# Value projection of the second 512 tokens in f16 high and low parts, K tiles outermost

## The chip, the cores and the metric

The kernel runs on one core of one Trainium2 chip. The metric is the device time of one launch in microseconds (us), where lower is better; times are medians of a few runs. The core has five engines, each of which takes its own instructions strictly in order: TensorE (matmuls; PE in the profile, its weight loads PEld), VectorE (DVE), ScalarE (ACT), GpSimd (POOL) and SyncE (SP). In this kernel SP issues nearly all DMA transfers, one after another, so a transfer that waits for its buffer holds up every later transfer in SP's order.

## The reference

One encoder layer on 1024 tokens of width 1024. A projection feeds two groups of attention heads, each group's output is gated, and an output projection, a residual and a layer norm follow:

```python
h = jnp.einsum('bsd,de->bse', x, w_in[layer])
q_a, k_a, v_a, z_a, q_b, k_b, v_b, z_b = jnp.split(h, SPLIT_POINTS, axis=-1)
y_a = neighborhood_attention(q_a, k_a, v_a, rel_pos_bias[layer])     # 8 heads of 64, 2-D window
y_b = windowed_gqa_with_sink(rotary(q_b), rotary(k_b), v_b, sink_logits[layer])
mixed = jnp.concatenate([y_a * jax.nn.silu(z_a), y_b * jax.nn.silu(z_b)], axis=-1)
y = jnp.einsum('bse,ed->bsd', mixed, w_out[layer])
x = layer_norm(DEEPNORM_ALPHA * x + y, ln_gain[layer], ln_bias[layer])
```

(The reshapes to heads are left out here.) All inputs and outputs are float32. What matters here is the first line, and of its columns the values v_a (512) and v_b (128): x (1024 x 1024) times 640 columns of w_in, called wv in the kernel.

## The kernel before, in words

**Number formats.** A float32 product is made of three products of narrower parts: with x = xh + xl and w = wh + wl, it takes xh wh + xl wh + xh wl. The parts are either fp32r (a rounded float32 that TensorE takes directly; in the profile f32), or f16 after scaling by a power of two that is made from the largest magnitude or the sum of magnitudes of the tensor.

**Value product.** The first stage (lines 402 to 587) computes the values, tokens as output rows, 640 columns in two parts of 320 (index a). K, the inner dimension, is 8 tiles of 128 (index k). x comes transposed, in two halves of 512 tokens; a half has four row tiles of 128 tokens (index t, 0 to 3 in the first half and 4 to 7 in the second). `load_x` and `load_wv` load a K tile into a staging buffer (`xr`, four; `wvr`, three), ACT casts it to the high fp32r part and DVE subtracts to get the low part. `v_mms` issues the three passes for one bank. For the first half k runs outermost over eight PSUM banks (four t by two a). For the second half (line 564) the bank runs outermost: one bank after another takes all 24 matmuls, and `v_out` then copies it on ACT to `v32`. The order of instructions in this stage and up to the output stage is the order in which the code is written (`manual_schedule`), for every engine.

**Scale of x.** The later projections take x in f16. `x_max` takes the largest magnitude of each of 16 x tiles on DVE; `x_scale`, in the second half's second group of matmuls, makes the common scale xsc with the help of a transposing matmul. All 16 x tiles are loaded a second time (`x2_load`), and `x16_part` makes their f16 parts: ACT the high part, and the low part DVE in one instruction or POOL in two.

**Weights of the projections.** Blocks of 128 columns of w_in, each in two halves of four K tiles (index m, block n has halves 2n and 2n+1). `w_load` brings a half into one of five buffers `wr`; `w_scan` sums its magnitudes on ACT; `w_scale(n)` turns the sums of block n into a scale, with a small matmul over the sums (line 222) that waits for both scans; `w_split` makes the f16 parts (ACT high; POOL low in two instructions, lines 201 and 202), and the load of half m+5 waits until POOL is done with half m, as it takes its buffer. Before, `w_split(0)` and `w_split(1)` stand within the second half of the value product (line 585).

**Projections.** `project` (line 355) computes one block for all tokens: two halves of 512 tokens, 24 matmuls of 512 columns each (line 376), alternating between two banks `pj`; ACT evacuates. Beside the first six, `run_to` runs events at fixed counts of matmuls: `v_scale` at 16 (a transposing matmul and small DVE steps for the scale of the values), `v_part(t)` from 30 on (values to f16, and out to DRAM), and `sum_w(i)` at 14, 28 and so on: it sums the magnitudes of a whole later block, loaded by `sum_load` as `ws` (512 KB), on ACT or DVE. The first four `ws` loads follow in SP's order the loads of weight halves 5 and 6. After that the attention runs beside the remaining projections.

Of the kernel before, what the change touches and what calls it, by code (L numbers as in the profile page):

```python
# [7 lines left out]
F32 = mybir.dt.float32  # L8
# [29 lines left out]
X1AT = 4  # L38
# [22 lines left out]
def hybrid_block(ctx, tc, xT, x, wt, wv, wo, bias, sink, gain, lbias, cos, sin, bmask, out):  # L61
# [27 lines left out]
    for half in range(2):  # L89
        for k in range(KT):  # L90
            t = big_tile(f"x{half}{k}")
            xh[half, k], xl[half, k] = t[:, 0, :], t[:, 1, :]
# [20 lines left out]
    xsc = const.tile([128, 1], F32, name="xsc")  # L113
    xrs = const.tile([128, 1], F32, name="xrs")
# [287 lines left out]
    with ExitStack() as vctx:  # L402
        vp = vctx.enter_context(tc.tile_pool(name="vp", bufs=2))
        vw = vctx.enter_context(tc.tile_pool(name="vw", bufs=1))
        wvh, wvl = [], []
        ps = bank("t")
        for _ in range(26):
            nc.tensor.matmul(ps[:, :128], warm, warm, start=True, stop=True)

        def load_x(half, k, cuts=(0, 512)):  # L410
            raw = vp.tile([128, 512], F32, tag="xr", name="xraw", bufs=4)
# [10 lines left out]
        def load_wv(k, cuts=(0, 640)):  # L422
            raw = vp.tile([128, 640], F32, tag="wvr", name="wvraw", bufs=3)
# [10 lines left out]
            for a, b in zip(cuts, cuts[1:]):  # L434
                nc.vector.tensor_sub(l[:, a:b], raw[:, a:b], h[:, a:b].bitcast(F32))
                yield

        def first_tiles():
            xr = vp.tile([128, 512], F32, tag="xr", name="xraw", bufs=4)
            wr = vp.tile([128, 640], F32, tag="wvr", name="wvraw", bufs=3)  # L440
# [16 lines left out]

        def interleave(*gens):
# [4 lines left out]
        def v_mms(ps, t, a, k, passes=(0, 1, 2)):  # L463
            ts = slice(128 * (t % 4), 128 * (t % 4) + 128)
            cs = slice(320 * a, 320 * a + 320)
            for i in passes:
                lh, rh = ((xh, wvh), (xl, wvh), (xh, wvl))[i]
                nc.tensor.matmul(ps[:, :320], lh[t // 4, k][:, ts], rh[k][:, cs],  # L468
                                 start=(k == 0 and i == 0), stop=(k == KT - 1 and i == 2))
# [3 lines left out]
        gm = const.tile([128, 1], F32, name="gm")  # L473

        def x_max(half, k):
            i = 8 * half + k
            nc.vector.tensor_reduce(xm[:, i:i + 1], xh[half, k].bitcast(F32), axis=AXX, op=ALU.max,
                                    apply_absolute_value=True)

        staged = [0]  # L480

        def stage(name):
            tag = ("xr", "xr", "xr", "xr", "wvr", "wvr", "wvr", "vt", "vt", "vt")[staged[0] % 10]
            staged[0] += 1
            if tag == "xr":
                return vp.tile([128, 512], F32, tag="xr", name=name, bufs=4)
            return vp.tile([128, 640], F32, tag=tag, name=name, bufs=3)[:, :512]

        def x_scale():
            ps = bank("t")  # L490
            nc.tensor.transpose(ps[:, :128], gm.to_broadcast([128, 128]), identf)
            nc.vector.tensor_reduce(gm, ps[:, :128], axis=AXX, op=ALU.max)
            nc.vector.tensor_scalar_max(gm, gm, 2.0 ** -16)
# [760 lines left out]
```

## Time and profile before

| | |
|---|---|
| median of 3 runs | 451.86 us (450.78 to 452.11) |
| the profiled execution, its own time | 451.96 us |
| its span in the profile | 450.2 us |
| matmuls | 3290 |
| TensorE busy | 440.9 us (98%) |
| DVE, ACT, POOL busy | 342.8, 301.6, 230.7 us |
| granted TensorE clock, mean | 0.999 of full speed |

In the profile a row of a timeline gives the start and the length in us, the engine, the line of the kernel, the operation, what is written from what is read, and shapes; in brackets stands how long the engine had been idle and what ended that. Matmul lengths overlap, since they are pipelined, so their cost is read from the distance of their starts. Where only the length of a run of equal instructions is given (x13), its share is the length divided by the count. "DMA to landing" is the time from issue to the last byte.

### The profile page before, as it was taken

To read this page: it belongs to the slowest core of one execution; us is meant where nothing else is said; L and a number is where in the kernel's file an instruction comes from. 1 tells how busy PE (TensorE), PEld (TensorE's weight loads), DVE (VectorE), ACT (ScalarE), POOL (GpSimd) and SP (SyncE) were. 2 spreads that over 40 slices of the span, in tenths; PEclk is the share of its full clock that TensorE was granted. 3 is DMA by queue.
4 is the path that set the end of the run, shared out by engine and by line. 5 is a ranking of instruction groups with operands and counts; after the bars stand their busy time and mean duration, and the time that the engine had idled before them with its cause. 6 is when DMAs were issued, how large, how long until landed. Compare 5 with 4: busy or idle time off the path is not lost.

```text
span 450.2 us, 9537 instructions
## 1 busy us (share of the span) xinstructions
PE 440.9 (98%) x3290; PEld 264.2 (59%) x3290; DVE 342.8 (76%) x833; ACT 301.6 (67%) x686; POOL 230.7 (51%) x241
## 2 busy tenths in 40 slices
PE   8999999999999999999999999999999999999994
PEld 8999974444445565555555555656556654444453
DVE  4787956628987797897888887888778837679944
ACT  4648649776489977787867888788778946302401
POOL 0003943555838558768506667765493504305740
PEclk9999999999999999999999999999999999999999
DMA  7898277975649999697778899989999988203611
GB/s 238 278 313 295 87 256 232 336 266 221 202 106 216 194 177 175 126 154 146 138 143 181 166 176 162 225 189 190 195 182 247 190 169 333 79 0 99 228 71 71
DMA packets 135281, 83.88 MB, mean 186 GB/s; under 512 B 101440, under 2 KB 113600, under 8 KB 134976
## 3 DMA queue, kind: packets, MB, share of 16 engines
q1 hardware_dynamic: 135088, 83.13, 76.9%
q8 instruction: 26, 0.43, 0.4%
q14 instruction: 23, 0.19, 0.1%
q10 hardware_dynamic: 144, 0.13, 0.1%
HBM read 52.83 MB, written 9.96 MB: 139 GB/s over the span
## 4 chain that ended last, share of the span: by engine, by line
PE 79%; DVE 6%; ACT 5%; issue 4%; DMA 3%; POOL 1%; SPq 0%; DVEq 0%; ACTq 0%; POOLq 0%
PE ps_pj L376 37%; PE ps_s L960 9%; PE ps_s L468 6%; PE ps_pj L960 5%; PE ps_t L810 5%; PE ps_t L960 5%; PE ps_pj L468 3%; PE ps_t L468 3%; PE ps_s L745 3%; PE ps_s L746 3%; ACT split L781 1%; DMA tr<-split 1%; DVE split L782 1%; ACT ps_s L771 1%; DMA wor<-in_wo 1%
## 5 line engine op out<-in xcount | busy, mean ns | idle before, releaser
L376 PE MATMUL ps_pj<-xf,wh 128*128 128x512 f16 x672 | 202.1, 379 | 0.3 <-DVE ks L260 0.3
L376 PE MATMUL ps_pj<-xf,wl 128*128 128x512 f16 x336 | 127.3, 379 | 0.0
L376 PEld LDWEIGHTS <-wh 128*128 128x128 f16 x672 | 63.6, 98 | 60.6 <-DVE ks L260 0.6
L771 ACT ACTIVATE ps_s<-sn,nm 128x385 f32<-128x385 f32 (+3 forms) x128 | 70.1, 548 | 28.4 <-DVE nm L755 28.0
L782 DVE SCALAR_TENSOR_TENSOR split<-ps_s,split 128x384 f16<-128x384 f32 (+2 forms) x128 | 65.7, 513 | 28.1 <-ACT split L781 26.4
L960 PEld LDWEIGHTS <-m 128*128 128x128 f16 x432 | 40.1, 98 | 41.1 <-DVE m L868 0.2
L781 ACT ACTIVATE split<-ps_s 128x384 f16<-128x384 f32 (+2 forms) x128 | 57.8, 452 | 3.3 <-DMA tr<-split 0.9
L376 PEld LDWEIGHTS <-wl 128*128 128x128 f16 x336 | 32.8, 98 | 37.4
L201 POOL TENSOR_SCALAR wr<-wr,wsc 128x512 f32<-128x512 f32 x26 | 20.7, 795 | 42.6 <-ACT wh L196 36.2
L960 PE MATMUL ps_s<-wo,m 128*128 128x512 f16 (+1 forms) x192 | 40.8, 366 | 0.0
L755 DVE CUSTOM_DVE_ANT_0 sn<-ps_s,bm,nsk 128x384 f32<-128x384 f32 (+1 forms) x64 | 40.6, 635 | 0.3
L745 PE MATMUL ps_s<-ks,qs 128*128 128x384 f16 (+4 forms) x128 | 39.2, 306 | 0.6 <-DVE qs L260 0.3
L755 DVE CUSTOM_DVE_ANT_0 sn<-ps_s,bias,sg 128x264 f32<-128x264 f32 (+1 forms) x64 | 35.0, 548 | 5.7 <-PE ps_s L746 2.7
L746 PE MATMUL ps_s<-ks,qs 128*128 128x384 f16 (+4 forms) x128 | 39.2, 306 | 0.0
L810 PEld LDWEIGHTS <-tr 128*128 128x128 f16 (+1 forms) x1104 | 36.7, 98 | 3.2 <-DMA tr<-split 0.6
L202 POOL TENSOR_TENSOR wl<-wr,wh 128x512 f16<-128x512 f32 x26 | 32.7, 1256 | 2.2
L717 POOL TENSOR_SCALAR bias<-bias,rsg 128x552 f32<-128x552 f32 (+1 forms) x24 | 19.1, 798 | 27.3 <-DMA bias<-in_bias 16.7
L292 POOL COPY ks<-ks 64x512 f16<-64x512 f16 x40 | 26.1, 661 | 7.3 <-DVE ks L260 2.8
L468 PE MATMUL ps_s<-wvh,x 128*128 128x320 f32 x128 | 29.8, 313 | 0.0
L1015 ACT ACTIVATE sd<-mv,eps 128x1 f32<-128x1 f32 x8 | 2.4, 294 | 36.0 <-DVE mv L1013 34.6
L1059 POOL TENSOR_TENSOR xr<-xr,gb 128x512 f32<-128x512 f32 x7 | 9.8, 1397 | 32.4 <-ACT xr L1056 32.4
L960 PE MATMUL ps_pj<-wo,m 128*128 128x512 f16 (+1 forms) x144 | 26.2, 326 | 0.0
(169 smaller groups left out, 823.4 us busy)
## 6 DMA issues: line engine op xcount, KB each, us to landing
xraw<-in_xT SPq DMA_DIRECT2D x31, 256.0 KB, 4.7
ws<-in_wt SPq DMA_DIRECT2D x15, 512.0 KB, 6.0
wr<-in_wt SPq DMA_DIRECT2D x26, 256.0 KB, 3.3
wor<-in_wo SPq DMA_DIRECT2D x22, 256.0 KB, 3.4
bias<-in_bias SPq DMA_DIRECT2D x16, 276.0 KB, 3.3
xr<-in_x SPq DMA_DIRECT2D x8, 512.0 KB, 9.6
out<-xr SPq DMA_DIRECT2D x15, 256.0 KB, 2.2
bias<-in_bias SPq DMA_DIRECT2D x8, 368.0 KB, 3.8
```

Of the source, the lines that this page charges most:

```text
L202: nc.gpsimd.tensor_sub(l, raw, h)
L292: nc.gpsimd.tensor_copy(t[o, sl], t[a, sl])
L376: nc.tensor.matmul(ps, a[:, k % 4, :], mv, start=(k == 0 and i == 0), stop=(k == KT - 1 and i == 2))
L468: nc.tensor.matmul(ps[:, :320], lh[t // 4, k][:, ts], rh[k][:, cs], start=(k == 0 and i == 0), stop=(k == KT - 1 and i == 2))
L745: nc.tensor.matmul(ps[:, :m], q, sl[0], start=True, stop=False)
L746: nc.tensor.matmul(ps[:, :m], q, sl[1], start=False, stop=True)
L755: nc.vector.tensor_tensor_reduce(sn[:, :m], ps[:, :m], bias_t, sg[:, c:c + 1], init, op0=ALU.add, op1=ALU.min, accum_out=nm)
L771: nc.scalar.activation(pt[:, :m], sn[:, :m], AF.Exp, bias=nm, scale=-1.0, accum_out=sm[:, k:k + 1])
L781: nc.scalar.activation(hl[:, :m, 0, :c], src, AF.Copy, scale=PSCALE)
L782: nc.vector.scalar_tensor_tensor(hl[:, :m, 1, :c], src, PSCALE, hl[:, :m, 0, :c], op0=ALU.mult, op1=ALU.subtract)
L810: nc.tensor.matmul(ps[:, HD * m:HD * m + HD], a, b_, start=(i == 0), stop=(i == len(mms) - 1))
L960: nc.tensor.matmul(ps, lh[:, ts], rh[:, cs], start=(e == EO[0] and i == 0), stop=(e == EO[-1] and i == 2))
```

## The change

- The four row tiles of the second half are multiplied from f16 parts: of x (`x16h`, `x16l`, the same ones that the projections use), and of wv (`wv16`, new, kept in the buffers of the gates z). The result is multiplied by the product of both units, `vdq`, in `v_out`.
- x's second half is loaded once, straight into its big tiles as float32 (`x1_load`), and never cast to fp32r. Its f16 parts are made from there. Of the first half, K tiles 4 to 7 stay in their staging buffers until their f16 parts are made, and tiles 0 to 3 are loaded again (`x0_again`).
- wv: six staging buffers instead of three, so that tiles 2 to 7 stay; tiles 0 and 1 are loaded again (`wv_again`). `wv_sum` sums the magnitudes of each tile on ACT; `wv_hi` (ACT) and `wv_lo` (DVE) make the f16 parts. For tiles 2, 4, 6 and 7 the low fp32r part moves from DVE to POOL.
- Both scales are made ahead of the second half, by `pow2` on DVE alone, in place of `x_scale` and its matmul.
- In the second half k runs outermost, in the order `KO`, over six banks (row tiles 4, 5 and 7); row tile 6 follows, two banks one after another.
- In the first half the passes run outermost over the four row tiles (k from 1 to 6), and x is loaded ahead of wv.
- `w_split(0)` and `w_split(1)` and the f16 parts of x's first tiles 1 to 3 stand in the last two groups of matmuls; the loads of cos and sin move behind the value product.

```diff
-X1AT = 4
+KO = (2, 3, 4, 5, 6, 7, 0, 1)
+X1_AT = ((), (), (0,), (1,), (2, 3), (4, 5), (6, 7), ())
...
+        def wv_stage(k):
+            nst[0] += 1
+            return vp.tile([128, 640], F32, tag=("wvr", "vt")[(nst[0] - 1) // 3 % 2], name="wvraw", bufs=3)
...
-                nc.vector.tensor_sub(l[:, a:b], raw[:, a:b], h[:, a:b].bitcast(F32))
+                (nc.gpsimd if k in (2, 4, 6, 7) else nc.vector).tensor_sub(l[:, a:b], raw[:, a:b], h[:, a:b].bitcast(F32))
...
+        def wv_sum(k):
+            nc.scalar.activation(junk[:, :640], wvh[k].bitcast(F32), AF.Abs, accum_out=wvm[:, k:k + 1])
...
-                lh, rh = ((xh, wvh), (xl, wvh), (xh, wvl))[i]
-                nc.tensor.matmul(ps[:, :320], lh[t // 4, k][:, ts], rh[k][:, cs],
-                                 start=(k == 0 and i == 0), stop=(k == KT - 1 and i == 2))
+                if t < 4:
+                    lh, rh = ((xh[0, k], wvh[k]), (xl[0, k], wvh[k]), (xh[0, k], wvl[k]))[i]
+                else:
+                    (xa, xb), (wa, wb) = (x16h[1, k], x16l[1, k]), wv16[k]
+                    lh, rh = ((xa, wa), (xb, wa), (xa, wb))[i]
+                ko = KO if t >= 4 else range(KT)
+                nc.tensor.matmul(ps[:, :320], lh[:, ts], rh[:, cs],
+                                 start=(k == ko[0] and i == 0), stop=(k == ko[-1] and i == 2))
...
+        def pow2(c, parts, op, least):
...
+            nc.vector.tensor_reduce(g, parts, axis=AXX, op=op)
+            nc.vector.tensor_copy(ta, g.to_broadcast([128, 32]))
+            nc.vector.transpose(tb, ta)
+            for b in range(4):
+                nc.vector.tensor_reduce(m4[:, b:b + 1], tb[32 * b:32 * b + 32], axis=AXX, op=ALU.max)
+            nc.vector.tensor_reduce(g[:32], m4, axis=AXX, op=ALU.max)
+            nc.vector.tensor_scalar_max(g[:32], g[:32], least)
+            nc.vector.tensor_scalar(g[:32].bitcast(I32), g[:32].bitcast(I32), 0x7F800000, None, op0=ALU.bitwise_and)
+            for b in range(4):
+                nc.vector.tensor_scalar_mul(unit[32 * b:32 * b + 32, c:c + 1], g[:32], 2.0 ** -14)
+            nc.vector.reciprocal(runit[:, c:c + 1], unit[:, c:c + 1])
...
+        def wv_hi(k):
+            nc.scalar.activation(wv16[k][0], wraw[k], AF.Copy, scale=wvs)
+
+        def wv_lo(k):
+            h, l = wv16[k]
+            nc.vector.scalar_tensor_tensor(l, wraw.pop(k), wvs, h, op0=ALU.mult, op1=ALU.subtract)
+            if k in (2, 3):
+                wv_again(k - 2)
...
-            if k in (1, 3) or (half, k) == (0, 5):
+            if k % 2 == 0:
                 nc.gpsimd.tensor_scalar(raw, raw, xsc, 1.0, op0=ALU.mult, op1=ALU.mult)
                 nc.gpsimd.tensor_sub(l, raw, h)
             else:
                 nc.vector.scalar_tensor_tensor(l, raw, xsc, h, op0=ALU.mult, op1=ALU.subtract)
+            if not half and k >= 4:
+                x0_again(k - 4)
...
+            for j in X1_AT[k]:
+                x1_load(j)
+            wv_sum(k)
+            x_max(0, k)
+            for j in X1_AT[k - 1] if 0 < k < 7 else ():
+                x_max(1, j)
...
+        pow2(1, wvm, ALU.add, 2.0 ** -30)
+        x_max(1, 6)
+        x_max(1, 7)
+        pow2(0, xm, ALU.max, 2.0 ** -16)
+        nc.vector.tensor_mul(vdq, unit[:, 0:1], unit[:, 1:2])
+
+        def ahead(i):
+            if i < KT:
+                k = KO[i]
+                wv_lo(k)
+                x16_part(1, k)
+                if i + 2 < KT:
+                    wv_hi(KO[i + 2])
+
+        wv_hi(KO[0])
+        wv_hi(KO[1])
+        ahead(0)
+        for i in (0, 2, 6, 1):
+            v_out(banks[i], i // 2, i % 2)
+        ahead(1)
+        for i in (3, 7):
+            v_out(banks[i], i // 2, i % 2)
+        ahead(2)
+        for i in (4, 5):
+            v_out(banks[i], i // 2, i % 2)
         for m in range(5):
             w_load(m)
...
+        for i, k in enumerate(KO):
+            ahead(i + 3)
+            if 1 <= i < 5:
+                w_scan(i - 1)
+            if i >= 3:
+                x16_part(0, (i + 1) % KT)
+            for a in range(2):
+                for t in (0, 1, 3):
+                    v_mms(part[2 * t + a], 4 + t, a, k)
+            if i in (4, 6):
+                w_scale(i // 2 - 2)
+            if i >= 4:
+                v_max(i - 4)
+        for t in (0, 1, 3):
+            for a in range(2):
+                v_out(part[2 * t + a], 4 + t, a)
...
+        for a in range(2):
+            ps = bank(tags[4 + a])
+            for k in KO:
+                v_mms(ps, 6, a, k)
+            if a == 0:
+                x16_part(0, 1)
+                w_split(0)
+                x16_part(0, 2)
+                v_max(4)
+            else:
+                x16_part(0, 3)
+                v_max(5)
+                v_max(7)
+                w_split(1)
+            v_out(ps, 6, a)
+        v_max(6)
...
         at(16, v_scale)
+        at(20, table_load, "cos", cos, "zc")
+        at(20, table_load, "sin", sin, "zs")
```

115 lines of the change are left out of this document (39 added, 76 removed).

## The prediction

> **What bounds the kernel now.** I read the page's busy shares first, then the chain that ended last (by engine, then in order of time), then the windows of the two stretches which the change touches: the second row block of the value product (33.29 to 61.90) and the first two projections behind it. In a window row the columns are length, busy time of PE, PEld, DVE, ACT and POOL with their counts, granted clock, DMA share and GB/s.
>
> ```profile
> span 450.2 us, 9537 instructions
> PE 440.9 (98%) x3290; PEld 264.2 (59%) x3290; DVE 342.8 (76%) x833; ACT 301.6 (67%) x686; POOL 230.7 (51%) x241
> PE 79%; DVE 6%; ACT 5%; issue 4%; DMA 3%; POOL 1%; SPq 0%; DVEq 0%; ACTq 0%; POOLq 0%
> ...
> 55.02 7.04 PE ps_s L468 x48
> 71.26 10.38 PE ps_pj L376 x48
> ...
> 33.29:61.90 28.61, 28.61 (x197) 28.17 (x195) 23.97 (x43) 17.90 (x37) 16.64 (x14) 1.00 0.59 194
> 61.90:82.50 20.60, 20.60 (x100) 9.49 (x99) 13.60 (x28) 18.57 (x33) 8.70 (x8) 1.00 0.86 277
> ```
>
> TensorE is busy in 98% of the span and holds 79% of the chain. In the value product 48 matmuls of 320 columns take 7.04 us, 146.7 ns each; in a projection 48 of 512 columns take 10.38, 216.2 ns each. No other engine ends a wait in either stretch, but ACT is busy in 18.57 of 20.60 us right behind the value product. So time can be won by cheaper matmuls, and any wait that TensorE gets here is paid in full, because it works without slack up to the tail.
>
> ```profile
> 8.08 0.31 PE L468 MATMUL ps_pj<-wvh,x 128*128 128x320 f32 x1
> 8.70 0.41 PE L468 MATMUL ps_pj<-wvh,x 128*128 128x320 f32 x1 [0.31 <-DVE x L419]
> ...
> 33.29 0.46 PE L468 MATMUL ps_pj<-wvh,x 128*128 128x320 f32 x2
> ...
> 61.90 0.60 PE L376 MATMUL ps_pj<-xf,wh 128*128 128x512 f16 x2
> ...
> 71.09 0.17 PE L222 MATMUL ps_t<-wm,ones 128*128 128x2 bf16 x1
> ```
>
> These are TensorE's own marks: its one wait in the first row block (8.08 to 8.70, for the low part of x's second K tile), the end of the first block (33.29), the first projection (61.90), and the small matmul that sums the statistics of the third weight block (71.09, 9.19 after 61.90).
>
> **Removed: time per matmul.** The second block's 192 matmuls change from fp32r to f16. The trace has no f16 matmul of 320 columns; it has 384 and 512.
>
> ```profile
> 200.48 0.33 PE L745 MATMUL ps_s<-ks,qs 128*128 128x384 f16 x1
> 200.64 0.33 PE L746 MATMUL ps_s<-ks,qs 128*128 128x384 f16 x1
> 200.81 0.59 PE L376 MATMUL ps_pj<-xf,wh 128*128 128x512 f16 x2
> ...
> L376 PEld LDWEIGHTS <-wh 128*128 128x128 f16 x672 | 63.6, 98 | 60.6 <-DVE ks L260 0.6
> L468 PEld LDWEIGHTS ps_s<-wvh,x 128*128 128x128 f32 x128 | 21.8, 190 | 0.0
> ```
>
> 384 columns start 0.16 to 0.17 us apart, 512 columns 0.216; the line through both gives 137 ns for 320. Weight loads are no obstacle: 98 ns in f16, 190 in fp32 (there they are longer than the matmul spacing, and overlap only in part). 192 x (146.7 - 137) = 1.86 us saved. Bounds: 2.6 (133 ns, if spacing goes with columns from 0.16 at 384) and 0 (if nothing but columns counted before).
>
> The Trainium skill (TensorE: Matmul & The Clock Gate, "Back-to-back issue gap") gives a sustained 131 ns for 512 columns and 81 for 128; by it 320 columns would cost about 106 ns, an estimate, and the saving would be near 7.8 us. The 216.2 ns measured here for 512 columns contradict it, so this stays out of the sum.
>
> In the first block x is now loaded ahead of wv, and all four row tiles take the high pass before the low one, so the low part of tile 1 has four matmuls more to arrive. The 8.70 start becomes 8.08 + 0.15: 0.47 us saved (0 to 0.47), and the first block ends near 32.8. The eight casts and eight subtractions of x's second half go away on ACT and DVE, which costs or saves nothing by itself, beside TensorE's work; the one matmul that made x's scale goes too, uncounted.
>
> **Added: a wait between the blocks.** Before, the second block needed only x's fp32r parts; the common scale of x was made beside it. Now every second-block matmul needs the scales of x and wv first. DVE must finish the subtraction of x's last first-half tile, then seven maxima, the power-of-two chain of wv, the last two maxima, and the same chain for x; then ACT casts tile 2, and POOL makes its low part, which the very second matmul needs.
>
> ```profile
> 18.00:20.00 2.00, 2.00 (x16) 2.00 (x15) 1.90 (x3) 1.89 (x4) 0.00 (x0) 1.00 0.48 179
> ...
> 20.82 0.62 ACT L416 CAST x<-xraw 128x512 fp32r<-128x512 f32 x1
> 33.13 0.79 ACT L526 COPY v<-ps_t 128x320 f32<-128x320 f32 x2
> 39.61 2.56 ACT L514 ACTIVATE xf<-xraw,xsc 128x512 f16<-128x512 f32 x4 [0.80 <-DVE xsc L496]
> ...
> 18.84 1.89 DVE L419 TENSOR_TENSOR x<-xraw,x 128x512 fp32r<-128x512 f32 x3
> 30.05 7.80 DVE L477 TENSOR_REDUCE xm<-x 128x1 f32<-128x512 f32 x13
> 40.37 0.75 DVE L519 SCALAR_TENSOR_TENSOR xf<-xraw,xsc,xf 128x512 f16<-128x512 f32 x1 [0.79 <-ACT xf L514]
> 43.34 0.15 DVE L225 TENSOR_SCALAR wg<-wg 128x1 int32<-128x1 int32 x1
> 43.53 0.15 DVE L226 TENSOR_SCALAR wsc<-wg 128x1 int32<-128x1 int32 x1
> 43.60 0.20 DVE L227 TENSOR_SCALAR inv<-wg,xrs 128x1 f32<-128x1 f32 x1
> 73.14 0.88 DVE L607 SCALAR_TENSOR_TENSOR vt<-v,vrs,vt 128x640 f16<-128x640 f32 x1
> ...
> 41.05 0.69 POOL L516 TENSOR_SCALAR xraw<-xraw,xsc 128x512 f32<-128x512 f32 x1 [39.74 <-ACT xf L514]
> 41.83 1.56 POOL L517 TENSOR_TENSOR xf<-xraw,xf 128x512 f16<-128x512 f32 x1
> 45.61 1.13 POOL L516 TENSOR_SCALAR xraw<-xraw,xsc 128x512 f32<-128x512 f32 x1
> 63.24 0.69 POOL L201 TENSOR_SCALAR wr<-wr,wsc 128x512 f32<-128x512 f32 x1 [4.98 <-ACT wh L196]
> 64.02 1.16 POOL L202 TENSOR_TENSOR wl<-wr,wh 128x512 f16<-128x512 f32 x1
> ```
>
> The tile k=7 was cast at 20.82. Two more x tiles go ahead of it in SP's order and wv of k=7 goes behind, while the loads no longer wait for three staging slots (at 18 to 20 the queue moved 179 GB/s at half load); I put the subtraction at 20.8 (19.9 to 22.0). It takes 0.63 (1.89 for three), seven maxima 0.60 each (7.80 for 13): 25.6. ACT's column sums of wv are done by then: two casts and a sum are about 3 x 0.8 = 2.4 us a tile (0.64 from 2.56 for four, times 640/512), while TensorE spends 24 x 146.7 = 3.5 on one. A power-of-two chain is nine dependent small steps, 0.19 apart (43.34 to 43.53), and six independent ones at 0.07 (43.53 to 43.60): 2.1; with the 32-wide copy and transpose, for which no row stands, 2.2 (2.1 to 15 x 0.19 = 2.85). So 27.8, two maxima 29.0, second chain 31.2. ACT's cast: 0.64 (2.56 for four): 31.85. POOL: 0.78 from 41.05 to 41.83 and 1.56: 34.2. Its bounds are 1.94 (63.24 to 64.02, plus 1.16) and 2.77 (1.13, 0.08 between, 1.56), because DVE runs the two wv low parts beside it.
>
> TensorE could go on at 32.8. The first matmul finds its bank, scale and high parts about in time; the second waits until 34.2: **1.3 us lost** (0 to 4.2 with all bounds on one side). Behind it one K tile is 18 x 137 = 2.47 us of TensorE; each needs from ACT two casts of 0.64 and 0.8, from DVE a 640-wide product-subtract (0.88) and every second time a 512-wide one (0.75), from POOL every second time 2.34. All fit, DVE even if they stretch by half. The eight bank evacuations are placed just ahead of the banks' use. These operations cost nothing as long as that cover holds; without it each would delay a K tile by its own length.
>
> **Moved: the first two weight splits, and what stands behind them on SP.** Before, they were made amid the second block. Now they stand in its last 6.6 us (48 matmuls for row tile 6). On SP the loads of weight halves 5 and 6 wait for them (slots of halves 0 and 1), and behind those wait the first four whole-block loads for the statistics (ws), then everything later on SP, cos and sin included. ACT, in order, takes the sum over ws 0, then an activation table load, the evacuation of the first projection bank and the sum of weight half 5; TensorE's small matmul needs that last one.
>
> ```profile
> 56.37 2.26 SPq L185 DMA_DIRECT2D wr<-in_wt  x2
> 59.01 1.93 SPq L623 DMA_DIRECT2D ws<-in_wt  x4
> ...
> DMA to landing us min/median/max: 3.7/5.2/6.9
> ...
> 64.27 1.04 ACT L631 ACTIVATE junk<-ws 128x1024 bf16<-128x1024 f32 x1
> 65.42 1.28 ACT L335 ACT_TABLE_LOAD   x1
> 67.41 0.69 ACT L335 ACTIVATE z<-ps_pj,inv 128x512 f32<-128x512 f32 x1 [0.70 <-PE ps_pj L376]
> 68.60 1.53 ACT L615 ACTIVATE vt<-v,vrs 128x640 f16<-128x640 f32 x2
> ```
>
> When the six-bank loop ends, ACT still has about 1.0 us of evacuations (0.79 for two), one x cast 0.64 and the weight cast 0.64: POOL starts at 2.3. Weight half 0: 1.94; x tile 2: 2.34; half 1: 1.94; done at 8.5, 1.9 us into the projection (1.4 to 3.6). Before, SP had both loads out at 56.37 + 2.26 = 58.63, 3.3 us ahead of the projection. TensorE itself needs half 1 only at 14 x 0.216 = 3.0. The ws issue follows about 0.8 later, at 2.7: the issue of half 6 (0.48 at the most, the pitch of the four) and 0.38 (58.63 to 59.01). Landing takes 3.7 at the least and 5.2 in the middle; only one transfer is ahead, so 4.1: 6.8 (before: issue 2.9 us ahead of the projection, so it was there when ACT came at 64.27). ACT then needs 65.42 - 64.27 = 1.15, 1.28 of table load, and 68.60 - 67.41 = 1.19: 3.6 in all, and TensorE may go on at 10.4. It gets there at 9.2: **1.2 us lost** (0.3 to 4). Further sums wait less: the other ws loads follow at 0.48 (1.93 for four), and ACT and TensorE are late together.
>
> The copies saved or added in DMA (12 x reloads fewer, two wv reloads more, cos and sin after the value product) lie beside TensorE's work; without that cover one load is worth its issue-to-landing time once, 3.7 to 5.2 by the row above.
>
> **Sum.** -1.86 - 0.47 + 1.3 + 1.2 = +0.2 us against the profiled execution's 451.96 (span 450.2 and 1.76 around it), which lies 0.10 over the median of 451.86. Forecast for the median: **452.1**, its own range 450.8 to 453.3.
>
> **Rivals.**
> 1. Both waits are hidden: the loads come 1 us earlier, and ws lands in 3.7 behind clean POOL work. Then only the savings stay: 451.86 - 2.3 = 449.5. For it: loads no longer stall on slots. Against: DVE's queue is fixed work from 21 on, and half 1 cannot be split earlier. With the first wait alone gone, 450.8.
> 2. Slower: the scale of x comes late. Start at 22.0, chains at 2.85, POOL at 2.77 give +2.9: 455.0. It decides as soon as x's scale is later than about 30 (then POOL's part is late), and from there each us costs one. For it: 30 small steps stand on one engine. A middle form is POOL fully blocked by each of DVE's two 0.88 us operations: 1.94 + 1.76 = 3.7 instead of 2.34, time 453.5. Against: clean and contended rows differ by 0.44 and 0.40, not by 0.88. The Trainium skill (SBUF — State Buffer, "Who interferes with whom") has just this exclusive lock between VectorE and GpSimd, the loser blocking for the whole instruction; the rows bear it out in direction only.
> 3. The second wait is longer, with ws landing 5.2 after issue and POOL contended: +2.7, 454.8.
> 4. The f16 matmul is no faster: 454.0. Against it stands the weight-load row.
>
> **How the numbers follow.** About 0.3% (1.36 us) is what a measurement can tell from no change. Forecast 0.43, rival 1 0.15 (half of it only partly so), rival 2 0.22, rival 3 0.15, rival 4 0.05. Faster by over 0.3% (below 450.5): 0.12 of rival 1 and 0.06 of the forecast's edge, 0.18. Slower (above 453.2): most of rivals 2 to 4, 0.38. Same: 0.44. Range 449.9 to 455.0.
>
> **What would show it.** Right: second-block matmuls 137 ns apart; TensorE's idle before the second one released by POOL's low part of tile 2, 1 to 2 us; the first projection at 60 to 61; idle before the statistics matmul released by ACT, with ACT's idle before the sum over ws ended by a DMA. Wrong: 147 ns spacing; a gap released by ACT's evacuation or by x's scale alone; no gap 9.2 us into the projections; a loss beyond 90 us.

## The result, and the profile after

| | kernel before | changed kernel |
|---|---|---|
| median, measured side by side | 451.10 us (448.43 to 452.17, 22 runs) | 452.43 us (449.89 to 455.62, 22 runs) |
| ratio | 1 | 1.0038 (95% interval 1.0020 to 1.0057) |
| profiled execution, its own time | 451.96 us | 455.62 us |
| its span | 450.2 us | 453.6 us |

The change costs 1.3 us in the median. It also widens the spread, and the profiled execution is the longest of its 22, so its trace shows more loss than a usual execution has. A second one is read below beside it. The page of the changed kernel:

```profile
span 453.6 us, 9544 instructions
PE 440.8 (97%) x3289; PEld 255.9 (56%) x3289; DVE 343.3 (76%) x851; ACT 308.0 (68%) x702; POOL 241.7 (53%) x251
PEclk9996999999999999999999999999999999999999
```

TensorE is busy as long as before, in a longer span, and the row of granted clocks, which was even before, has a 6 in its fourth slice. TensorE's timeline shows the marks that the prediction used:

```profile
32.60 0.31 PE L486 MATMUL ps_s<-wvl,x 128*128 128x320 f32 x1
35.78 0.34 PE L486 MATMUL ps_pj<-wq,xf 128*128 128x320 f16 x1 [2.87 <-ACT v L560]
37.39 0.71 PE L486 MATMUL ps_pj<-wq,xf 128*128 128x320 f16 x2 [1.27 <-POOL xf L546]
...
59.48 6.68 PE L486 MATMUL ps_t<-wq,xf 128*128 128x320 f16 x48
66.00 0.59 PE L379 MATMUL ps_pj<-xf,wh 128*128 128x512 f16 x2
...
76.63 0.16 PE L225 MATMUL ps_t<-wm,ones 128*128 128x2 bf16 x1 [1.29 <-ACT junk L219]
```

The last matmul of the first block starts at 32.60, so the block ends about 0.15 later, at 32.75 (before: 33.29). Then TensorE waits 2.87 us for ACT's evacuation of bank 0, does one matmul, and waits 1.27 for POOL's low part of x: 4.14 us between the blocks. Row tile 6's 48 matmuls take 66.00 - 59.48 = 6.52 us, 135.8 ns each. From the second matmul of the block to the first projection pass 66.00 - 37.39 = 28.61 us, where 191 matmuls at 135.8 ns need 25.94: 2.67 us are lost with no wait shown. The windows (length, PE busy, granted clock, DMA share, GB/s) say where:

```profile
35.50:36.00 0.50, 0.22 (x1) 0.91 0.54 97
36.00:42.50 6.50, 5.22 (x21) 0.50 0.94 318
42.50:43.00 0.50, 0.50 (x5) 0.77 0.34 111
```

The mean of 0.91 in the first window puts the fall to half clock at 35.91 us, and the mean of 0.77 in the last puts its end at 42.73. TensorE works through 5.34 us of that, from 37.39 on, and half of 5.34 is the 2.67. The statistics matmul, which stood at 71.09 before, is at 76.63: 5.54 us late. That is -0.54 (first block) - 2.1 (192 matmuls at 146.7 - 135.8 ns) + 4.14 + 2.67 + 1.29 = 5.5. The span is only 3.4 us longer, so 2.1 us come back further on.

Why the scale of x is late stands in the timelines of VectorE, GpSimd and ScalarE:

```profile
20.94 1.57 POOL L445 TENSOR_TENSOR wvl<-wvraw,wvh 128x640 fp32r<-128x640 f32 x1 [1.58 <-ACT wvh L442]
21.02 2.04 DVE L429 TENSOR_TENSOR x<-xraw,x 128x512 fp32r<-128x512 f32 x1
22.98 4.23 DVE L494 TENSOR_REDUCE xm<-x 128x1 f32<-128x512 f32 x7
27.14 0.14 DVE L504 TENSOR_REDUCE g<-wvm 128x1 f32<-128x8 f32 x1
27.77 0.74 DVE L508 TENSOR_REDUCE m<-tb 32x1 f32<-32x32 f32 x4
29.08 0.62 DVE L513 TENSOR_SCALAR unit<-g 32x1 f32<-32x1 f32 x4
33.73 0.16 DVE L514 RECIPROCAL runit<-unit 128x1 f32<-128x1 f32 x1
...
33.98 0.72 ACT L543 ACTIVATE xf<-x,runit 128x512 f16<-128x512 f32 x1 [2.50 <-issue]
34.61 0.81 ACT L524 ACTIVATE wq<-wvraw,runit 128x640 f16<-128x640 f32 x1
35.33 0.40 ACT L560 COPY v<-ps_pj 128x320 f32<-128x320 f32 x1
...
34.80 1.30 POOL L545 TENSOR_SCALAR x<-x,runit 128x512 f32<-128x512 f32 x1 [12.29 <-ACT xf L543]
36.18 1.15 POOL L546 TENSOR_TENSOR xf<-x,xf 128x512 f16<-128x512 f32 x1
```

VectorE's last subtraction of x takes 2.04 us. POOL's subtraction of wv began 0.08 us before it and ends at 22.51; VectorE ends 0.55 after that. The seven maxima end at 27.14, each chain of small steps takes 2.7 us, and x's scale is there at 33.8. ACT makes x's high part and another tile of wv, and then first evacuates bank 0, though that bank was full before 31. POOL's low part is ready at 37.33.

The second wait, on SP, POOL and ACT:

```profile
64.34 4.59 SPq L188 DMA_DIRECT2D wr<-in_wt  x2
67.42 1.16 POOL L205 TENSOR_TENSOR wl<-wr,wh 128x512 f16<-128x512 f32 x1
68.98 1.96 SPq L686 DMA_DIRECT2D ws<-in_wt  x4
72.82 1.06 ACT L694 ACTIVATE junk<-ws 128x1024 bf16<-128x1024 f32 x1 [4.26 <-DMA ws<-in_wt]
73.99 1.28 ACT L338 ACT_TABLE_LOAD   x1
```

SP's second weight load waits for POOL (68.58), the ws loads follow at 68.98, and ACT stands idle for 4.26 us until the first has landed. Then come ACT's sum over it, a table load of 1.28 us, an evacuation, and the sum (line 219) that the statistics matmul needs.

### The profile page after: what moved, and what is told of

Its sections match the earlier page's. It is cut to its first block, busy times and chain, and to the rows that moved or that the text cites. A ratio compares the mean times of both kernels' runs of the same rounds, so it can differ in the third digit from the quotient of the medians.

```text
span 453.6 us, 9544 instructions
## 1 busy us (share of the span) xinstructions
PE 440.8 (97%) x3289; PEld 255.9 (56%) x3289; DVE 343.3 (76%) x851; ACT 308.0 (68%) x702; POOL 241.7 (53%) x251
## 4 chain that ended last, share of the span: by engine, by line
PE 75%; issue 6%; ACT 5%; POOL 5%; DMA 4%; DVE 4%; SPq 0%; POOLq 0%; ACTq 0%; DVEq 0%
PE ps_pj L379 38%; PE ps_s L1025 9%; PE ps_t L875 6%; PE ps_pj L1025 5%; PE ps_t L1025 5%; PE ps_s L810 3%; PE ps_s L811 3%; PE ps_s L486 3%; DMA xraw<-in_xT 2%; PE ps_pj L486 2%; DMA wvraw<-in_wv 1%; PE ps_t L895 1%; POOL wl L205 1%; ACT ps_s L836 1%; ACT split L846 1%
## 5 line engine op out<-in xcount | busy, mean ns | idle before, releaser
L486 PEld LDWEIGHTS <-xf 128*128 128x128 f16 x192 | 19.6, 103 | 13.3 <-POOL xf L546 2.5
```

Of the source, the lines that this page charges most:

```text
L486: nc.tensor.matmul(ps[:, :320], lh[:, ts], rh[:, cs], start=(k == ko[0] and i == 0), stop=(k == ko[-1] and i == 2))
```

## The experiments

An execution is called disturbed here if VectorE's last subtraction of x had to wait for POOL.

**1. The changed kernel once more.** No edit.

> The changed kernel once more, nothing edited. Theory A: it loses its time at two waits (4.1 us of TensorE idle between the two blocks, made up of a wait for the evacuation of bank 0 and one for GpSimd's low part; 1.3 us ahead of the statistics matmul), and in some executions, not in all, the granted clock falls to half behind the first of them, which costs up to 2.9 us more. Then the two waits come again within 0.3 us of 2.87, 1.27 and 1.29, the granted clocks of the executions spread (0.990 to 0.998), and the executions with a clock of 0.997 or more are 1 to 3 us shorter than those with 0.993 or less. Rival B: the low clock of the profiled execution was a state of that chip and has nothing to do with the wait: then the clocks of all executions here lie within 0.002 of each other, and the spread of the times is as small as that of the kernel before. Median by both: 1 to 2 us over the kernel before.

Median 452.62 us (12 runs), ratio 1.0051 (1.0024 to 1.0079). This profiled execution is not disturbed:

```profile
20.83 0.67 DVE L429 TENSOR_TENSOR x<-xraw,x 128x512 fp32r<-128x512 f32 x1
21.01 1.93 POOL L445 TENSOR_TENSOR wvl<-wvraw,wvh 128x640 fp32r<-128x640 f32 x1 [1.84 <-ACT wvh L442]
25.58 0.14 DVE L504 TENSOR_REDUCE g<-wvm 128x1 f32<-128x8 f32 x1
32.17 0.16 DVE L514 RECIPROCAL runit<-unit 128x1 f32<-128x1 f32 x1
...
34.23 0.30 PE L486 MATMUL ps_pj<-wq,xf 128*128 128x320 f16 x1 [1.37 <-ACT v L560]
35.84 0.72 PE L486 MATMUL ps_pj<-wq,xf 128*128 128x320 f16 x2 [1.31 <-POOL xf L546]
63.41 0.59 PE L379 MATMUL ps_pj<-xf,wh 128*128 128x512 f16 x2
74.75 0.16 PE L225 MATMUL ps_t<-wm,ones 128*128 128x2 bf16 x1 [2.00 <-ACT junk L219]
```

VectorE began 0.18 us ahead of POOL, took 0.67, and POOL took 1.93. The maxima end at 25.58, 1.56 us earlier than in the first trace, and TensorE's two waits shrink to 2.68. So, against the expectation, the first gate was not within 0.3 us of 2.87 but 1.5 shorter, about as much as the maxima were earlier, and the wait ahead of the statistics matmul was 2.00 instead of 1.29. The clock was halved here too: 63.41 - 35.84 - 25.94 = 1.63 us lost. The clocks of the executions spread from 0.987 to 0.999 (a fall at the very end alone, which the traces of both kernels show, makes 0.001 to 0.006 of that); in the first set the 7 executions with 0.996 or more have a median of 451.23 us, the other 15 one of 453.07. In 31 runs of the kernel before, clock and time are unrelated.

**2. Zero matmuls in the wait.**

```diff
+                        if k == KT - 1 and a == 1 and ts == (3,) and ps == (2,):
+                            for _ in range(44):
+                                nc.tensor.matmul(banks[7][:, :128], warm, warm, start=False, stop=False)
```

> 44 matmuls of the zero tile with itself (128 columns) are added into bank 7 before its last pass: they add nothing to it, and keep TensorE busy for about 2.5 us of the wait between the blocks. The waits themselves stay. Theory A: the granted clock stays at 1.00 between 33 and 66 us, first projection at 63.1 where the profiled execution of the changed kernel had 66.0, every execution at a clock of 0.997 or more, and the median 1.0 to 2.0 us below the changed kernel's. Rival B (the low clock has another cause): the clock falls again in some executions, median within 0.5 us of the changed kernel's. Rival C (what is lost ahead of 100 us is regained in waits further back, so nothing here reaches the end): the projection starts earlier and the median is still within 0.5 us.

In the profiled execution the clock stayed at 1.00 and the first projection came at 61.84, where an execution like that of 1 without its 1.63 us would have it (61.8). But theory A asked for a clock of 0.997 or more in every execution, and only two of the eight have it (one has 0.991, at 457.01 us); and the median was 453.03 us (8 runs), not lower. So one trace speaks for what theory A says of the clock, and its time is not met; 7 takes it up again.

**3. One chain for both scales.** The new `pow2` takes the same steps on tiles with two columns.

```diff
-        pow2(1, wvm, ALU.add, 2.0 ** -30)
         x_max(1, 6)
         x_max(1, 7)
-        pow2(0, xm, ALU.max, 2.0 ** -16)
+        pow2()
```

> The two chains of small VectorE operations that make the two scales become one over two columns (18 operations in place of 30), behind the last two maxima. By the rows of the changed kernel it ends 2.1 us earlier (31.7 in place of 33.9 us). Theory A (the wait between the blocks is the late scale of x, with ScalarE's three tiles and GpSimd's low part behind it): TensorE's idle time between the blocks falls from 4.1 to 2.0 to 2.6 us, the half clock comes more rarely or not at all, and the median is 1.5 to 3 us below the changed kernel's. Rival D (ScalarE's order decides: with the scale of the value weights later by 1.8 us in this form, its tiles start later, and the evacuation of bank 0 stands behind them): idle time 3.3 to 4.1, median within 1 us of the changed kernel's. Rival C (regained further back): idle time falls, median within 0.5 us.

Median 450.08 us (12 runs), 2.5 below the changed kernel beside it. The chain took 3.2 us (26.63 to 29.82). TensorE's waits:

```profile
33.09 0.30 PE L486 MATMUL ps_pj<-wq,xf 128*128 128x320 f16 x1 [0.32 <-ACT v L563]
34.25 0.45 PE L486 MATMUL ps_pj<-wq,xf 128*128 128x320 f16 x2 [0.86 <-POOL xf L549]
```

1.18 us in place of 2.68, in an execution that is not disturbed. The late scale is the cause of most of the first wait; rivals C and D fall. Low clocks came more rarely, but three of the twelve executions still have 0.990 to 0.993.

**4. Loads for the column sums ahead of the waiting weight loads.** The last f16 tile of x is reserved earlier for it, so that buffers keep their order.

```diff
                 x16_part(0, 1)
+                pre[2] = big_tile("xf02", (128, 2, 2, 512), F16)
+                for i in range(4):
+                    sum_load(i)
                 w_split(0)
                 x16_part(0, 2)
```

> The first four loads for the column sums go onto SP's queue ahead of the two weight loads that wait for GpSimd, so that they are issued before 62 us and land before the first projection is done. The wait between the blocks stays as it is. Theory A: the idle time ahead of the statistics matmul (1.29 us) falls below 0.2, and the projections behind it run 1.0 to 1.3 us earlier; the median falls by 0.6 to 1.3 us. Rival C: the 1.3 us vanish at 76 us but come back as waits before the end (the lag against the kernel before shrank from 5.5 to 3.4 us in the profiled execution), median within 0.4 us of the changed kernel's.

Median 450.52 us (12 runs), 2.1 below. The statistics matmul has no wait and stands 9.25 us behind the first projection (9.19 in the kernel before):

```profile
35.65 0.45 PE L486 MATMUL ps_pj<-wq,xf 128*128 128x320 f16 x2 [1.32 <-POOL xf L548]
61.65 0.59 PE L379 MATMUL ps_pj<-xf,wh 128*128 128x512 f16 x2
70.90 0.17 PE L225 MATMUL ps_t<-wm,ones 128*128 128x2 bf16 x1
```

The gain is more than the 0.6 to 1.3 us expected from the 1.29 of the first trace. In the seven traces that have this wait it is 1.29 to 2.08 us long; what is left of the 2.1 is within the uncertainty of such medians, whose ratios have intervals of about 1 us to either side. Rival C falls here too.

**5. The kernel before once more.** No edit.

> The kernel before once more, nothing edited. In its first profiled execution the statistics matmul of L222 that stands 9 us into the projections began at 71.09 us and the program ended at 450.2: 379.1 us. In the five profiled executions with the change that stretch took 375.4 to 377.0 us. Theory F: the stretch differs from execution to execution (in the stretches 165 to 185 and 319 to 335 us, where the lags jump) and owes nothing to the change; then it takes 375.5 to 377.5 us here too and the statistics matmul stands at 71.1 within 0.3. Rival G: the change shortens it; then it takes 378.6 to 379.6 again. By both the granted clock of nearly all executions is 0.994 or more.

Its statistics matmul stood at 71.50 and the span is 449.3: 377.8 us from there to the end, between the two theories. The eleven profiled executions with the change took 375.3 to 377.2 for this stretch, the two of the kernel before 379.1 and 377.8. So 0.6 to 3.8 us come back in it, by which two traces are compared; the first trace of the kernel before is itself a long execution, 451.96 us against a median of 451.10. Part of it differs by execution, as one wait in this trace that no other of the traces shows at this length:

```profile
162.69 0.35 PE L810 MATMUL ps_t<-vb,tr 128*128 128x64 f16 x6 [1.18 <-DMA tr<-split]
```

What the rest is was not settled.

**6. The two gates of the first wait, one at a time.** First only ScalarE's order:

```diff
+        v_out(banks[0], 0, 0)
         wv_hi(KO[0])
         wv_hi(KO[1])
         ahead(0)
-        for i in (0, 2, 6, 1):
+        for i in (2, 6, 1):
```

> Only ScalarE's order between the blocks is edited: the evacuation of bank 0 stands ahead of the tiles that need the scales, in place of behind four of them. Theory A (two gates, one behind the other: bank 0's evacuation, then GpSimd's low part of x): the first matmul of the second block comes at 33.2 to 33.5 us where the undisturbed execution had 34.23, but the second still waits for GpSimd until 35.8, so the sum of the two waits stays at 2.5 to 2.8 us (4.0 to 4.3 if VectorE's last subtraction loses to GpSimd's in the profiled execution), and the median stays within 0.7 us of the changed kernel's 452.5. Rival H (the evacuation is the gate that decides, and GpSimd's part would be in time without it): the sum falls to 1.3 to 1.7 us.

Then only the engine of the low part of K tile 2:

```diff
-            if k % 2 == 0:
+            if k % 2 == 0 and (half, k) != (1, 2):
                 nc.gpsimd.tensor_scalar(raw, raw, xsc, 1.0, op0=ALU.mult, op1=ALU.mult)
```

> Only the low part of x's first tile of the second block moves from GpSimd (two operations, 1.30 and 1.16 us) to VectorE (one, about 0.75 us, behind the two low parts of the value weights). Theory A: the first gate stays (idle 1.37 us by an undisturbed execution, 2.87 by a disturbed one), the second falls from 1.31 to 0.2 to 0.5 us, because the low part is there at 34.8 in place of 35.8; median 0.5 to 1.5 us below the changed kernel's. Rival H: nothing changes in the sum of the waits.

With bank 0 first, the median was 452.07 us (10 runs), ratio 1.0024 (1.0002 to 1.0047); with the low part on VectorE 451.15 (10 runs), 1.0011 (0.9987 to 1.0035). TensorE's waits of both kernels, the first kernel's in the first fence:

```profile
33.81 0.31 PE L486 MATMUL ps_pj<-wq,xf 128*128 128x320 f16 x1
36.28 0.45 PE L486 MATMUL ps_pj<-wq,xf 128*128 128x320 f16 x2 [2.15 <-POOL xf L546]
```

```profile
33.78 0.57 PE L486 MATMUL ps_pj<-wq,xf 128*128 128x320 f16 x3 [0.40 <-ACT v L560]
36.41 0.98 PE L486 MATMUL ps_s<-wq,xf 128*128 128x320 f16 x6 [0.85 <-ACT v L560]
```

With bank 0 out of the way the whole wait goes over to POOL's low part; it ended 3.5 us behind x's scale as in 1 (here 32.77 and 36.22). The sum, 2.15, is under the expected 2.5 because the first block ended 1.1 us later in this execution, the scale 0.45 later. With the low part on VectorE the second gate is gone, and what is left is ACT's evacuations, 1.25 us in all; that the first of them is down from 1.37 to 0.40 is in part a first block that ended 0.5 us later. Both medians are as theory A expected. POOL's part was the gate that decided; the evacuation in front of it cost nothing of its own, and becomes the gate when POOL's is removed.

**7. Zeros again, with the second wait gone.** The edits of 4 and of 2, with 52 zero matmuls.

> The early loads for the column sums together with 52 zero matmuls (about 3 us of work that adds nothing) into bank 7 ahead of its last pass. With the second wait gone, the only place in which the granted clock can fall for lack of work ahead of 100 us is the wait between the blocks, and the zeros cover it. The early loads alone had a median of 450.52 us, with clocks of 0.989 to 0.998, and over their 12 executions the span grew by 5 us for each 0.01 of clock. Theory A (the half clock behind the wait is what makes most executions longer): no clock below 0.993 (a fall in the last 50 us, which the kernel before has too, makes up to 0.006), median 448.8 to 449.8 us. Rival B (the low clocks come from elsewhere; the zeros alone did not lower the median): clocks down to 0.989 as before, median 450 to 451.5 us.

No execution has a clock below 0.995, where the early loads alone had 0.989 to 0.998. Windows of the profiled one, across the wait:

```profile
33.00:36.00 3.00, 3.00 (x54) 1.00 0.61 183
36.00:39.00 3.00, 3.00 (x24) 1.00 0.95 306
```

So the half clock comes from the idle stretch between the blocks. But the median is 450.47 us (12 runs) against 450.52: theory A's time fails for the second time. Some of it is the price of the zeros, since the second block started at 36.06 here and POOL's part was there at 35.53. And the times still run from 448.5 to 453.4 at full clocks, so a low clock need not be what makes a time long; a long wait may make both, but no run separates this. What the half clock costs in the median was not resolved; in the three traces that hold it, it cost 2.67, 1.63 and 1.74 us.

**8. Both edits of 3 and 4.**

> The one chain for both scales and the early loads together. Theory A (the two waits lie one behind the other on the path that sets the end, and neither is regained later): the gains add, 2.4 us (one chain) and 2.0 us (early loads) off the 452.5 us of the changed kernel, and so a median of 447.8 to 448.8 us; idle between the blocks 1.0 to 1.4 us, none ahead of the statistics matmul. Rival C (part of one gain is the other's): median 449.3 to 450.2.

Median 448.99 us (12 runs), ratio 0.9974 (0.9947 to 1.0002); idle between the blocks 1.15 us, none at the statistics matmul. That is 3.5 of the 4.4 us that the sum of both gains would give: most of it adds, nearer to theory A than to C, and a part does not. The interval, 2.5 us wide, does not separate the two.

**9. No POOL operation beside VectorE's last subtraction.**

```diff
-                (nc.gpsimd if k in (2, 4, 6, 7) else nc.vector).tensor_sub(...)
+                (nc.gpsimd if k in (2, 4, 6) else nc.vector).tensor_sub(...)
```

> The low part of the last K tile of the value weights moves from GpSimd to VectorE, so that GpSimd has no operation beside VectorE's last subtraction of x. In the profiled executions this subtraction took 2.04 us where GpSimd's 1.57 us operation had begun 0.08 us before it, and 0.67 us where it began 0.18 us before GpSimd's, which then took 1.93. Theory A (the two wait for one another, and the one that begins first goes first): the subtraction takes 0.67 to 0.70 us in any execution; VectorE has 0.8 us more to do, so the second chain ends at 32.7 to 33.2 us (32.25 undisturbed, 33.8 disturbed), the sum of the waits between the blocks is 3.2 to 3.8 us, median within 0.8 us of 452.5. Rival I (the 2.04 us have another cause, such as the cast that it reads or the load): it takes over 1 us here too in some look, and the chain ends at 34 or later.

```profile
17.66 1.57 POOL L445 TENSOR_TENSOR wvl<-wvraw,wvh 128x640 fp32r<-128x640 f32 x1 [1.99 <-ACT wvh L442]
18.08 1.70 DVE L429 TENSOR_TENSOR x<-xraw,x 128x512 fp32r<-128x512 f32 x1
...
20.89 0.68 DVE L429 TENSOR_TENSOR x<-xraw,x 128x512 fp32r<-128x512 f32 x1
32.97 0.16 DVE L514 RECIPROCAL runit<-unit 128x1 f32<-128x1 f32 x1
```

The last subtraction took 0.68 us, which alone says little, since the second trace had 0.67 without this edit. The one before it, which still had POOL's operation beside it, took 1.70: POOL's ended at 19.23, this one 0.55 later. The other traces say the same: in the eleven with the change 17 of VectorE's subtractions in the first block took over 1 us, and each ended 0.54 or 0.55 us behind one of POOL's; all others took less than 0.95. So rival I falls. The chain ended at 33.1, as expected. The waits were 2.80 us, less than expected, because the first block ended at 33.4; the median was 453.41 (10 runs), 0.9 over 452.5 and so just above what was expected. Giving VectorE the work costs at least as much as it avoids.

**10. All late steps taken out.** One chain, early loads, and this order between the blocks (`outs` evacuates banks):

```diff
+        outs(0)
+        wv_hi(2); wv_lo(2); x16_part(1, 2)
+        outs(2, 6); wv_hi(3); wv_lo(3)
+        outs(1, 3); x16_part(1, 3)
+        outs(7); wv_hi(4); wv_lo(4); x16_part(1, 4)
+        outs(4, 5); wv_hi(5); wv_hi(6)
...
-            if k % 2 == 0:
+            if k % 2 == 0 and (half, k) not in ((1, 2), (1, 4)):
```

> All that the theory names as late is taken out together: one chain for both scales, bank 0's evacuation ahead of the scale, the tiles of K tile 2 ahead of the other evacuations, the low parts of x for K tiles 2 and 4 on VectorE, the first four loads for the column sums ahead of the waiting weight loads. Theory A: TensorE idle between the blocks below 0.5 us, none ahead of the statistics matmul, granted clock 1.00 from 33 to 66 us, first projection at 58.8 to 59.6 (61.90 in the kernel before), all executions at a clock of 0.996 or more, median 447.5 to 449 us, that is 1.5 to 3 below the kernel before. Rival C (regained or lost again further back): projection as early, median above 449.8.

Median 447.42 us (12 runs) beside 450.47 for the kernel before (34 runs): ratio 0.9938 (0.9917 to 0.9959). It beats both kernels, by 3 and 5 us. TensorE:

```profile
34.71 0.45 PE L486 MATMUL ps_pj<-wq,xf 128*128 128x320 f16 x2 [0.66 <-DVE xf L553]
...
61.04 0.59 PE L379 MATMUL ps_pj<-xf,wh 128*128 128x512 f16 x2
...
70.91 0.17 PE L225 MATMUL ps_t<-wm,ones 128*128 128x2 bf16 x1
```

```profile
21.52 1.57 POOL L445 TENSOR_TENSOR wvl<-wvraw,wvh 128x640 fp32r<-128x640 f32 x1 [1.09 <-ACT wvh L442]
22.09 1.55 DVE L429 TENSOR_TENSOR x<-xraw,x 128x512 fp32r<-128x512 f32 x1
```

As the second fence shows, this execution was disturbed, and even so only 0.66 us of waiting was left there, a little more than expected; the projection came 1.4 us later than the latest time expected, partly for that and partly because the first block ended at 33.5. The lowest clock was 0.994, where 0.996 was expected. At the statistics matmul this execution is only 0.2 us ahead of the kernel before (70.91 against 71.09), at the end 3.3 (446.9 against 450.2). So most of what it gains on the kernel before comes behind that matmul, in the stretch that 5 left open. The gain over the changed kernel is of the size of what was taken away: 2.68 - 0.66 + 1.63 + 2.00 = 5.65 us by the second trace.

## Why the prediction was right or wrong

The forecast was +0.24 us against the median shown (452.1 against 451.86); the median measured, 452.43, lies 1.33 over the kernel before beside it; the ratio, 0.38% over 1, is just on the slower side of the 0.3% bound, with both sides in its interval. The range held it. That the sum came so near is in part luck. In the second trace the two waits and the half clock took 3.8 us more than it had for them, and 3.4 came back behind the statistics matmul, where it had nothing; in the first trace these are 5.6 and 2.1. By its own terms, in us, against the two traces (the last row is taken against the first trace of the kernel before; against the one of experiment 5 it is -0.8 and -2.1):

| step | predicted | first trace (disturbed) | second trace |
|---|---|---|---|
| wait in the first block gone | -0.47 | -0.54 | -0.59 |
| 192 f16 matmuls | -1.86 | -2.1 | -2.1 |
| wait between the blocks | +1.3 | +4.14 | +2.68 |
| half clock behind it | not in the sum | +2.67 | +1.63 |
| wait ahead of the statistics matmul | +1.2 | +1.29 | +2.00 |
| behind that matmul, to the end | 0 | -2.1 | -3.4 |

The second trace's span is thus only 0.3 us over that of the kernel before, but its own time, 453.22, is 1.3 over: 2.7 us of it lie outside the span, where most executions have 1.8.

**Right.** The spacing in f16 (137 ns predicted, 135.8 measured). The first block's end (32.8; 32.75 and 32.70). The second wait, in mechanism and nearly step by step: ws issued 2.98 us into the projection (2.7 predicted), landed at 6.8 (6.8), TensorE released at 10.63 (10.4), in the first trace; in the second ws was issued at 2.98 too, but landed at 7.5 and TensorE was released at 11.3. Experiment 4 removes it. The K tiles behind the first wait cost nothing beyond the clock: 191 matmuls take their 25.94 us, plus what the clock takes.

**Mis-sized: the wait between the blocks.** The mechanism was right, and experiment 6 confirms that POOL's low part of the second matmul sets it. By the second trace the maxima ended at 25.58 (25.6 predicted), but the second matmul started at 35.84 instead of 34.2. Of these 1.6 us, 1.06 are the two chains with the maxima between (32.26 against 31.2). A chain took 2.7, not 2.2: the prediction priced six of its steps at 0.07 us from a pair of rows (43.53 and 43.60), while four reductions on quarter slices take 0.74 together and four multiplications 0.62, 0.16 to 0.19 each. That is inside its upper bound of 2.85. The rest is ACT's tile and its handover (0.35) and POOL (0.2).

**Missed place: VectorE and GpSimd.** The change gives POOL four subtractions of wv beside VectorE's subtractions of x. The prediction bounded the start of the last one by 22.0 for late loads, and weighed the lock between the two engines in rival 2 only for the low part after the scale, where POOL in fact ran nearly as priced (2.53 against 2.34). Where it strikes is the subtraction before the maxima, which then ends 1.5 us later, and which decides by a tenth of a us: 20.83 against 21.01 in one execution, 21.02 against 20.94 in the other. It is not the usual case: of the ten traces that keep POOL's last subtraction of wv, two are disturbed, the first and that of experiment 10. The Trainium skill (SBUF — State Buffer, "Who interferes with whom") says that a VectorE operation with two inputs in SBUF shares a port with GpSimd's reads, that the one which begins first keeps it for its whole instruction, and that reductions stay clear of it. The traces agree: 0.55 us after POOL's end in every disturbed subtraction here (2.04, 1.70 and 1.55 us long), and the seven maxima took 4.23 in both cases.

**Missed term: the clock.** A wait was priced by its length alone. Experiments 2 and 7 show that the half clock follows from the idle time, and three traces give its price. In the first trace it lasted 6.82 us (35.91 to 42.73). In the second it lasted 3.41 (35.66 to 39.07), as the means of 0.66 and 0.93 in these windows give it:

```profile
35.50:36.00 0.50, 0.16 (x1) 0.66 0.84 246
39.00:39.50 0.50, 0.50 (x5) 0.93 0.90 291
```

With bank 0 first (experiment 6) it lasted 3.42 (37.07 to 40.49, from means of 0.57 in 37.0 to 37.5 and 0.51 in 40.0 to 40.5). Half of 3.41 is 1.71, near the 1.63 lost in the second trace and the 63.96 - 36.28 - 25.94 = 1.74 lost with bank 0 first. So the clock seems to be set anew every 3.41 us, and in the 3.41 us that ended with the fall TensorE had been idle for 2.87, 2.51 and 2.15 us. The Trainium skill (TensorE: Matmul & The Clock Gate, "Part 1: The HAM clock gate") has the clock halved after an idle window of about 3.4 us that runs free of the program. The length of the window and that it runs free fit the runs. That the 3.4 us must pass without any work does not fit: the clock fell with 2.15 us idle. Waits of 2.39 (experiment 4) and 2.80 us (experiment 9) did not halve it. In the first trace the clock's next fall, at 452.33, lies 409.60 us behind 42.73, which is 120 times 3.4133. Counted in such steps back from the next fall in the traces of experiments 4 and 9 (444.04 and 448.44 us), a window ended at 34.44 and at 35.43, just behind the single matmul between the two parts of the wait, so no window held more than 1.20 and 1.59 us of idle time. By these traces it is the idle time within one window that counts, and where the windows lie differs by execution. A run that moves a wait against the windows was not made.

**Wrong in a remark.** "The first matmul finds its bank ... about in time": it waited 1.37 and 2.87 us for its evacuation, which ACT takes behind four tiles that need the scales. It did not matter, as POOL's gate lay behind it. **Missed beyond 90 us:** the prediction had nothing there, and 0.6 to 3.8 us came back; the cause is open.

## What to carry to other kernels

Before a stage is made to depend on a global scale, count the small dependent operations that make it, price each from a row of the same shape, and handle several scales as columns of one tile. Work that moves to GpSimd is not free beside VectorE operations with two SBUF inputs: where one of them lies on the path to a wait, the loss depends on which starts first, and single executions differ by the length of an operation. Price a wait of TensorE with the clock behind it, and look in each engine's order for what does not need the late value and yet stands behind it: with one chain for both scales, earlier loads, two low parts on VectorE and such a new order, a kernel 1.3 us slower than before became one 3 us faster.

## What the runs showed of the hardware

- The same program ran with two outcomes, by the order in which VectorE and GpSimd began: 0.67 us and 1.93 us, or 2.04 and 1.57. All 17 VectorE subtractions of the first block that took over 1 us ended 0.54 or 0.55 us behind one of GpSimd's.
- Behind a wait the clock was halved for 6.82, 3.41 and 3.42 us. In the 3.41 us ahead of the fall TensorE had been idle for 2.87, 2.51 and 2.15 us. Waits of 2.39 and 2.80 us, of which no such window held more than 1.59, left the clock as it was, and so did 1.96 us in one window ahead of the statistics matmul in experiment 2. In the last 10 us of a launch, where matmuls are few, it also fell after windows with 1.8 to 1.9 us idle, so the limit is not sharp.
- VectorE operations on 32 partitions and one to 64 elements took 0.13 to 0.22 us each. Four on quarter slices started 0.16 to 0.19 us apart although none needs another, while two others that are independent started 0.07 apart (28.51 and 28.58 in experiment 3). With two columns in place of one they took hardly longer (0.88 against 0.74 us for four reductions).
